# A down projection with 16 of its 22 chunks by a seven-product scheme

## The chip, the core and the metric

The kernel runs on one core of a Trainium2 chip. The metric is the time of one execution on the device, in microseconds. Three runs of the kernel before gave 772.88, 773.05 and 773.07 us, a median of 773.05.

## What is computed

One layer of a decoder trunk on 512 tokens of 1024 channels, in float32: a mixer with two branches, an output projection, and a dense gated feed-forward network (FFN). The change touches the last matrix product, `w_down` with 2816 rows and 1024 columns:

```python
def swiglu(h, w_gate, w_up, w_down):
    return (jax.nn.silu(h @ w_gate) * (h @ w_up)) @ w_down

    ...
    h = rmsnorm(x, ffn_pre_g[l])
    x = x + rmsnorm(swiglu(h, w_gate[l], w_up[l], w_down[l]), ffn_post_g[l])
```

## The kernel before

Every operand of a large product is split into a high half, which is the value rounded to the format `fp32r`, and a low half, the rest. A product is then three matmuls: high by high, high by low, low by high (`mm3`, lines 153 to 156). The high half is a copy on ScalarE (ACT in the profile; line 70) and the low half a subtraction on VectorE (DVE; line 71). Both stand in the helper `split`.

The FFN's gate and up product already runs by Strassen's scheme with seven products per quad of weight blocks (`jobs`, `prep_job`, `product`, lines 672 to 862). Sums of weight blocks are made there by accumulating DMAs, which POOL issues (`add_to`, line 692), and by additions on VectorE. Its result is `act`, 22 tiles of 128 rows by 512 tokens.

The down projection follows. It runs over 22 chunks `kc` of 128 rows of `w_down`. `unit("d", kc)` gives the halves of a chunk's weights (128 x 1024, tiles `whi` and `wlo`, four buffers each) and `halves(kc)` those of `act[kc]`. For each chunk, `down` (lines 938 to 941) does four blocks of 128 tokens by two halves of 512 columns by three matmuls, 24 in all, into eight PSUM banks `db`. The stationary operand is a 128 x 128 piece of the activations and the moving one 512 columns of weights. A product's weights are prepared three units ahead of it (`AHEAD`). Weights come in as `raw` tiles of 512 KB through SP's DMA queue, four buffers deep.

The last four chunks (`RES`) are kept whole, and their matmuls are done token block by token block, so that each block's finish runs beside the next block's matmuls: a square with a row sum on ScalarE, a product with the gain on VectorE, an inverse root by three Newton steps (`rsqrt`, lines 158 to 180; on POOL, for the last block on VectorE), a scalar_tensor_tensor that scales and adds the residual, and the DMA out.

Engines take their instructions in order. The order on each is set by a scheduler that works from the order of the code; only instructions marked by `keep_in_program_order` are bound to it. Tiles of a pool that is opened where another was closed wait for the old tiles' last users.

Of the kernel before, what the change touches and what calls it, by code (L numbers as in the profile page):

```python
# [31 lines left out]
def trunk(ctx: ExitStack, tc: tile.TileContext, x, xt, w_n, w_f, w_u, w_ga, w_gb, w_qk,  # L32
          w_o, w_gq, w_d, pcol, b_f, w_sp, rows, out):
# [896 lines left out]

# [3 lines left out]
    stage["pool"], stage["n"] = dn, 14  # L934
    x2 = {}
    db = [[bank(f"d{tb}{i}") for i in range(2)] for tb in range(NT)]

    def down(kc, tb, i, w):
        o = slice(tb * P, (tb + 1) * P)
        c = slice(i * HALF, (i + 1) * HALF)  # L940
        mm3(db[tb][i], ath[kc][:, o], atl[kc][:, o], w[0][:, c], w[1][:, c], kc == 0, kc == NF - 1)

    for kc in range(NF - RES):
        halves(kc)
        w = unit("d", kc)
        halves(kc + 1)
        if kc == 2:
            g_fpost = row(3, "g_fpost")
        if 4 <= kc < 4 + NT:
            tb = kc - 4  # L950
            x2[tb] = []
            for i in range(2):
                t = slot(f"x2{tb}{i}")
                nc.sync.dma_start(out=t, in_=x2d[tb * P:(tb + 1) * P, i * HALF:(i + 1) * HALF])
                x2[tb].append(t)
        for tb in range(NT):
            for i in range(2):
                down(kc, tb, i, w)
    for kc in range(NF - RES, NF):
        halves(kc)  # L960
    last = [unit("d", kc) for kc in range(NF - RES, NF)]
    for tb in range(NT):
        end = tb == NT - 1
# [1 line left out]
        ts_ = [slot(f"dg{tb}{i}") for i in range(2)]
        for i in range(2):
            for kc in range(NF - RES, NF):
                down(kc, tb, i, last[kc - NF + RES])
# [1 line left out]
            nc.scalar.activation(out=j, in_=db[tb][i], func=AF.Square, accum_out=ss[:, i:i + 1])  # L970
            if end and i:
                nc.scalar.activation(out=ts_[i], in_=db[tb][i], func=AF.Copy)
                nc.gpsimd.tensor_tensor(out=ts_[i], in0=ts_[i], in1=g_fpost[i], op=ALU.mult)
            else:
                nc.vector.tensor_tensor(out=ts_[i], in0=db[tb][i], in1=g_fpost[i], op=ALU.mult)
# [61 lines left out]
```

## Time and profile before

| | us |
|---|---|
| median of three runs | 773.05 |
| profiled execution | 774.62 |
| its span, first to last instruction | 772.9 |
| TensorE busy in it | 754.0 |
| VectorE busy | 454.7 |
| ScalarE busy | 341.1 |
| POOL busy | 137.8 |

The times of the trace run from 0 to the span's 772.9 us. The down projection's first matmul starts at 645.42 us and its last at 764.90. PE is TensorE's matmuls, PEld its weight loads. "Idle before" is the time that an engine stood still before an instruction, with what ended it. A matmul's duration contains its way through the array, so the time between two starts tells more than the duration.

### The profile page before, as it was taken

How to read it: one execution, taken by the hardware profiler on the slowest of the kernel's cores; microseconds unless marked ns; L12 is line 12 of the kernel's file. 1: busy time of each engine (PE TensorE's matmuls, PEld its weight loads, DVE VectorE, ACT ScalarE, POOL GpSimd, SP SyncE). 2: the span in 40 equal slices, each digit the busy share in tenths (PEclk: the TensorE clock that was granted, in tenths of full speed). 3: DMA queues.
4: the chain of work that ended last, by engine and by line, in shares of the span. 5: the costliest groups of instructions: out<-in, count | busy, mean ns of one | idle time of the engine just before them, and what ended most of it. 6: DMA issues, size and time to landing. Idle time of an engine off the chain costs nothing. (4 is left out here: it accounts for less than half of the span.)

```text
span 772.9 us, 11042 instructions
## 1 busy us (share of the span) xinstructions
PE 754.0 (98%) x4294; PEld 663.3 (86%) x4294; DVE 454.7 (59%) x718; ACT 341.1 (44%) x561; POOL 137.8 (18%) x213
## 2 busy tenths in 40 slices
PE   8999999999999989999998899999999999999996
PEld 6888778888888878888888799999999998888884
DVE  4647732244325566776589599887778766334415
ACT  5343662322235544555468464444444545233312
POOL 0103000022024254444133201001010000000013
PEclk9999999999999999999999999999999999999999
DMA  8625332222232222231678769776877317332202
GB/s 293 226 72 186 114 107 93 98 82 83 84 121 96 68 96 96 74 104 56 198 291 297 199 206 262 209 191 181 206 194 184 83 58 250 129 109 87 77 0 109
DMA packets 34451, 109.55 MB, mean 142 GB/s; under 512 B 4568, under 2 KB 4824, under 8 KB 34400
## 3 DMA queue, kind: packets, MB, share of 16 engines
q1 hardware_dynamic: 30352, 94.82, 35.8%
q0 software_dynamic: 3168, 11.54, 8.6%
q10 hardware_dynamic: 880, 2.51, 0.8%
q8 instruction: 33, 0.54, 0.3%
q14 instruction: 18, 0.15, 0.1%
HBM read 104.64 MB, written 4.21 MB: 141 GB/s over the span
## 5 line engine op out<-in xcount | busy, mean ns | idle before, releaser
L154 PE MATMUL d<-whi_d,ath 128*128 128x512 f32 x144 | 56.0, 389 | 0.0
L155 PE MATMUL d<-wlo_d,ath 128*128 128x512 f32 x144 | 56.0, 389 | 0.0
L156 PE MATMUL d<-whi_d,atl 128*128 128x512 f32 x144 | 56.0, 389 | 0.0
L496 POOL TENSOR_SCALAR dm<-cb,cq 128x128 f32<-128x128 f32 (+3 forms) x32 | 40.0, 1259 | 74.4 <-DMA cb<-cdr 70.4
L692 POOL DMA_DIRECT2D a<-in_w_gq x22 | 19.2, 872 | 166.2 <-DVE s L721 49.4
L70 ACT ACTIVATE whi<-raw_a 128x1024 fp32r<-128x1024 f32 x29 | 30.6, 1058 | 28.3 <-issue 12.8
L71 DVE TENSOR_TENSOR wlo<-raw_a,whi 128x1024 fp32r<-128x1024 f32 x29 | 35.4, 1221 | 7.8 <-ACT whi L70 7.8
L71 DVE TENSOR_TENSOR atl<-act,ath 128x512 fp32r<-128x512 f32 x22 | 14.8, 691 | 42.6 <-ACT ath L70 42.6
L70 ACT ACTIVATE whi<-a 128x1024 fp32r<-128x1024 f32 x26 | 27.5, 1059 | 25.7 <-PE Y L861 10.9
L71 DVE TENSOR_TENSOR wlo<-s,whi 128x1024 fp32r<-128x1024 f32 x22 | 26.9, 1224 | 15.8 <-ACT whi L70 15.8
L70 ACT ACTIVATE ath<-act 128x512 fp32r<-128x512 f32 x22 | 13.3, 627 | 50.8 <-PE d L155 50.8
L70 ACT ACTIVATE whi<-s 128x1024 fp32r<-128x1024 f32 x22 | 23.3, 1060 | 27.5 <-PE V L861 19.2
L71 DVE TENSOR_TENSOR wlo<-a,whi 128x1024 fp32r<-128x1024 f32 x26 | 31.7, 1221 | 4.2 <-ACT whi L70 4.1
L453 POOL TENSOR_TENSOR sga<-sga,ug 128x512 f32<-128x512 f32 x8 | 14.1, 1761 | 99.7 <-ACT sga L442 99.7
L154 PEld LDWEIGHTS d<-whi_d,ath 128*128 128x128 f32 x144 | 27.0, 188 | 5.6
L155 PEld LDWEIGHTS d<-wlo_d,ath 128*128 128x128 f32 x144 | 27.0, 188 | 5.6
L156 PEld LDWEIGHTS d<-whi_d,atl 128*128 128x128 f32 x144 | 27.0, 188 | 5.5
L71 DVE TENSOR_TENSOR wlo_o<-raw_o,whi_o 128x512 fp32r<-128x512 f32 x32 | 21.1, 685 | 13.2 <-ACT whi_o L70 13.1
L861 PE MATMUL X<-b21h,whi 128*128 128x256 f32 x88 | 25.5, 290 | 2.8 <-ACT s L876 2.7
L71 DVE TENSOR_TENSOR wlo_d<-raw_d,whi_d 128x1024 fp32r<-128x1024 f32 x18 | 22.1, 1225 | 10.4 <-ACT whi_d L70 10.4
L71 DVE TENSOR_TENSOR wlo_ga<-raw_ga,whi_ga 128x1024 fp32r<-128x1024 f32 x8 | 9.8, 1225 | 29.9 <-ACT whi_ga L70 16.9
L70 ACT ACTIVATE whi_o<-raw_o 128x512 fp32r<-128x512 f32 x32 | 18.9, 624 | 18.4 <-PE o L156 7.7
(316 smaller groups left out, 2590.7 us busy)
## 6 DMA issues: line engine op xcount, KB each, us to landing
raw_a<-in_w_gq SPq DMA_DIRECT2D x36, 512.0 KB, 4.8
a<-in_w_gq SPq DMA_DIRECT2D x22, 512.0 KB, 6.5
a<-in_w_gq POOLq DMA_DIRECT2D x22, 512.0 KB, 6.8
raw_d<-in_w_d SPq DMA_DIRECT2D x22, 512.0 KB, 3.4
raw_o<-in_w_o SPq DMA_DIRECT2D x16, 512.0 KB, 3.2
raw_va<-in_w_n SPq DMA_DIRECT2D x8, 512.0 KB, 6.0
raw_u<-in_w_u SPq DMA_DIRECT2D x8, 512.0 KB, 3.3
raw_ga<-in_w_ga SPq DMA_DIRECT2D x8, 512.0 KB, 3.2
```

Source lines behind the costliest of these rows:

```text
L70: keep(nc.scalar.activation(out=hi, in_=src, func=AF.Copy))
L71: keep(nc.vector.tensor_tensor(out=lo, in0=src, in1=hi.bitcast(F32), op=ALU.subtract))
L154: nc.tensor.matmul(ps_ap, lh, rh, start=first, stop=False)
L155: nc.tensor.matmul(ps_ap, lh, rl, start=False, stop=False)
L156: nc.tensor.matmul(ps_ap, ll, rh, start=False, stop=last)
L453: nc.gpsimd.tensor_tensor(out=sg, in0=sg, in1=ug[j], op=ALU.mult)
L496: nc.gpsimd.tensor_scalar(out=dm[:, :n], in0=cb[:, :n], scalar1=cq[:, i, h:h + 1], scalar2=None, op0=ALU.subtract)
L692: tc.keep_in_program_order(nc.gpsimd.dma_start(out=t, in_=quad_of(g, n_), accum_op=ALU.add))
L861: nc.tensor.matmul(o, l_[:, w_], r_[:, kc, :], start=start and pair + kc + m == 0, stop=pair == 1 and kc == 3 and m == 2, skip_group_check ...
```

## The change

Sixteen of the 22 chunks form four quads `q` of four chunks. In a quad, rows are halved (chunks 0 and 2 against 1 and 3), weight columns are halved (2 x 512), and tokens are halved (2 x 256). That gives weight blocks a11, a12, a21, a22 of 128 x 1024 each and activation blocks b11 to b22. A quad takes seven products of 12 matmuls each in place of 96 matmuls. The products go pass by pass: pass 1 for the quads 0 to 3, then passes 2, 6, 7 and 5; pass 3 alternates with the six plain chunks 16 to 21 (`"s"`), two of which stand alone after it; pass 4 comes last. Below, 6q3 is the product of pass 6 for quad 3.

- Sums of weights: `load_sums` loads a11 and a21 of a quad through SP and adds a22 onto a21 by an accumulating DMA that POOL issues. In pass 6 VectorE adds a21 + a22 and a11 to s2 (`s2d`), and POOL then issues a second accumulating DMA, a21 onto a11. Pass 3 adds a12 onto s2 on VectorE. Of each quad, eight transfers of 512 KB take the place of four.
- Sums of activations: VectorE, in pieces of 128 x 256, in place in `act` or in `t2`.
- Each product splits its activation block in two pieces of 256 columns (`th`, `tl`).
- Results go to four pairs of banks, V, X, Y and Z. `kept` copies V to SBUF on ScalarE after passes 1, 6 and 5; `combine` merges these with X, Y and Z on VectorE.
- The end: after the last plain chunk, token blocks 2 and 3 are finished while pass 4 runs; then `finish` of block 0 and of block 1. The resident four chunks are gone, and so is the split of the last block's finish over ScalarE and POOL.

```diff
-    ath, atl, dn = [None] * NF, [None] * NF, None
-
-    def halves(kc):
-        if kc < NF and ath[kc] is None:
-            ath[kc], atl[kc] = (dn.tile([P, S], F32R, tag=n_, bufs=6, name=f"{n_}{kc}") if dn else
-                                slot(f"{n_}{kc}", F32R) for n_ in ("ath", "atl"))
-            split(ath[kc], atl[kc], act[kc])
+    DQ = 4
+    order_d = [(p, q) for p in "12675" for q in range(DQ)]
+    rest = list(range(4 * DQ, NF))
+    for q in range(DQ):
+        order_d += [("s", rest[q]), ("3", q)]
+    order_d += [("s", kc) for kc in rest[DQ:]] + [("4", q) for q in range(DQ)]
...
+    def load_d(k):
+
+        if k < len(order_d) and k not in draw:
+            p, q = order_d[k]
+            src = {"1": "a11", "2": "a12", "3": "a12", "4": "a22"}
+            if p in src or p == "s":
+                draw[k] = st.tile([P, D], F32, tag="raw", bufs=NRAW, name=f"raw_d{p}{q}")
+                nc.sync.dma_start(out=draw[k], in_=w_d[q - 4 * DQ] if p == "s" else dquad(q, src[p]))
+
+    def load_sums(q):
+        if q < DQ:
+            for n_ in ("a11", "a21"):
+                dtile[q, n_] = dn.tile([P, D], F32, tag="dq", bufs=3 * DQ, name=f"{n_}d{q}")
+                nc.sync.dma_start(out=dtile[q, n_], in_=dquad(q, n_))
+            nc.gpsimd.dma_start(out=dtile[q, "a21"], in_=dquad(q, "a22"), accum_op=ALU.add)
+
+    def prep_unit():
...
+        for k_ in range(k, k + 4):
+            load_d(k_)
+        if p == "2":
+            load_sums(q + 2)
+        add = lambda out, a_, b_, o=ALU.add: nc.vector.tensor_tensor(out=out, in0=a_, in1=b_, op=o)
+        if p == "s":
+            th, tl = (pair_tile(n_, 3, f"{n_}{q}") for n_ in ("ath", "atl"))
+            split(th, tl, act[q])
+            src = draw[k]
+        else:
+            half = lambda c, j: act[4 * q + c][:, j * 2 * P:(j + 1) * 2 * P]
+            if p == "6":
+                dtile[q, "s2"] = dn.tile([P, D], F32, tag="dq", bufs=3 * DQ, name=f"s2d{q}")
+                add(dtile[q, "s2"], dtile[q, "a21"], dtile[q, "a11"])
+                nc.gpsimd.dma_start(out=dtile[q, "a11"], in_=dquad(q, "a21"), accum_op=ALU.add)
+                t2s[q] = dn.tile([P, S], F32, tag="t2", bufs=DQ, name=f"t2d{q}")
+            if p == "3":
+                add(dtile[q, "s2"], dtile[q, "s2"], draw[k])
...
+                if p == "6":
+                    t = t2s[q][:, o]
+                    nc.vector.scalar_tensor_tensor(out=t, in0=b11, scalar=-1.0, in1=b22,
+                                                   op0=ALU.mult, op1=ALU.subtract)
+                elif p == "7":
+                    add(b12, b12, b22, ALU.subtract)
+                elif p == "4":
+                    add(b21, b21, t2s[q][:, o])
+                split(th[:, o], tl[:, o], t)
+                if p == "2":
+                    add(b11, b11, b12, ALU.subtract)
+        hi = st.tile([P, D], F32R, tag="whi", bufs=4, name=f"whi_d{p}{q}")
+        lo = st.tile([P, D], F32R, tag="wlo", bufs=4, name=f"wlo_d{p}{q}")
+        split(hi, lo, src)
...
+    def d_part(k, i, q=None):
...
+        for r in range(2):
+            t_ = slice(r * 2 * P + i * P, r * 2 * P + (i + 1) * P)
+            w_ = slice(r * HALF, (r + 1) * HALF)
+            for m, (l_, r_) in enumerate(((th, wh), (th, wl), (tl, wh))):
+                nc.tensor.matmul(b, l_[:, t_], r_[:, w_], start=p in "127" and q + r + m == 0,
...
+    combine("s", X, ALU.add)
+    combine("v5", Z, ALU.add)
+    for i in range(2):
+        finish(2 + i, (lambda: V[i], lambda: held["v5"][i]), False)
+    while dstate["next"] < len(order_d):
+        prep_unit()
+    for i in range(2):
+        for k in range(first4, len(order_d)):
+            d_part(k, i)
+
+        def tail():
+            if not held.get(("done", i)):
+                add(held["v"][i], Y[i], held["v"][i], ALU.subtract)
+                held["done", i] = True
+            return held["v"][i]
+
+        finish(i, (lambda: held["s"][i], tail), i == 1)
```

Where the instructions stand. First POOL, from the FFN's last accumulating DMA on (`a` is an FFN weight tile, `v_d`, `y_d`, `w_d` and `t_d` are the inverse root's), before:

```order
L692 DMA a_5893<-in_w_gq 128x1024
L164 TENSOR_SCALAR v_d_7045<-sd_7012 128x1
L168 TENSOR_SCALAR y_d_7046<-v_d_7045 128x1
L170 TENSOR_SCALAR w_d_7047<-v_d_7045 128x1
L173 TENSOR_SCALAR t_d_7048<-y_d_7046,w_d_7047 128x1
```

and now, with the quads 0 to 3 as tiles 6380, 6385, 6424, 6453 of a21 and 6378, 6383, 6422, 6451 of a11:

```order
L685 DMA a_5893<-in_w_gq 128x1024
L905 DMA a21d_6380<-in_w_dq 128x1024
L905 DMA a21d_6385<-in_w_dq 128x1024
L905 DMA a21d_6424<-in_w_dq 128x1024
L927 DMA a11d_6378<-in_w_dq 128x1024
L927 DMA a11d_6383<-in_w_dq 128x1024
L905 DMA a21d_6453<-in_w_dq 128x1024
L927 DMA a11d_6422<-in_w_dq 128x1024
L927 DMA a11d_6451<-in_w_dq 128x1024
L157 TENSOR_SCALAR v_d_7244<-sd_7236 128x1
```

Eight accumulating DMAs now stand ahead of the first inverse root, and a21 of quad 3 stands behind a11 of quads 0 and 1.

VectorE in pass 6, now, from the low half of 2q3's weights to the low half of 6q3's (`wlo_d_6629`); before, this stretch held only low halves of weights and activations in turn:

```order
L71 TENSOR_TENSOR wlo_d_6517<-raw_d_6420,whi_d_6516 128x1024
L71 TENSOR_TENSOR tl_6537<-t2d_6535,th_6536 128x256
L917 TENSOR_TENSOR s2d_6532<-a21d_6380,a11d_6378 128x1024
L71 TENSOR_TENSOR tl_6537<-t2d_6535,th_6536 128x256
L917 TENSOR_TENSOR s2d_6560<-a21d_6385,a11d_6383 128x1024
...
L917 TENSOR_TENSOR s2d_6616<-a21d_6453,a11d_6451 128x1024
L71 TENSOR_TENSOR tl_6621<-t2d_6619,th_6620 128x256 x2
L71 TENSOR_TENSOR tl_6645<-act_3734,th_6644 128x256
L71 TENSOR_TENSOR tl_6645<-act_3801,th_6644 128x256
L71 TENSOR_TENSOR wlo_d_6629<-s2d_6616,whi_d_6628 128x1024
```

The sum `s2d_6616` of quad 3 and four short subtractions stand ahead of 6q3's low half.

VectorE at the end, before, from the last low half of weights (`wd_7009`) on:

```order
L71 TENSOR_TENSOR wd_7009<-raw_d_6874,wd_7009 128x1024
L71 TENSOR_TENSOR atl_7002<-act_6118,ath_7001 128x512
L71 TENSOR_TENSOR atl_7006<-act_6291,ath_7005 128x512
L975 TENSOR_TENSOR dg_7013<-d_6370,g_fpost_6452 128x512
L975 TENSOR_TENSOR dg_7014<-d_6371,g_fpost_6454 128x512
L982 SCALAR_TENSOR_TENSOR dg_7013<-dg_7013,y_d_7046,x_6524 128x512
```

and now, with 4q3's low half as `wlo_d_7295`:

```order
L1053 TENSOR_TENSOR dg_7262<-v5d_6908,g_fpost 128x512
L1053 TENSOR_TENSOR dg_7262<-Vd_6389,g_fpost 128x512
L1058 SCALAR_TENSOR_TENSOR dg_7237<-dg_7237,y_d_7245,x_7128 128x512 x2
L1058 SCALAR_TENSOR_TENSOR dg_7262<-dg_7262,y_d_7270,x_7070 128x512 x2
L71 TENSOR_TENSOR wlo_d_7295<-raw_d_7130,whi_d_7294 128x1024
L1053 TENSOR_TENSOR dg_7323<-sd_6504,g_fpost 128x512
L1053 TENSOR_TENSOR dg_7373<-sd_6505,g_fpost 128x512
L867 TENSOR_TENSOR vd_6716<-Yd_6392,vd_6716 128x512
L1053 TENSOR_TENSOR dg_7323<-vd_6716,g_fpost 128x512
L1058 SCALAR_TENSOR_TENSOR dg_7323<-dg_7323,y_d_7332,x_7230 128x512 x2
L867 TENSOR_TENSOR vd_6717<-Yd_6393,vd_6717 128x512
```

The last low half of weights stood ahead of every finish; now it stands behind the finish of token blocks 2 and 3 (`dg_7237`, `dg_7262`), and block 1's subtraction (`vd_6717`) stands behind block 0's finish.

TensorE in pass 4, now, where bank 6392 is token block 0's and 6393 block 1's; 18 matmuls of 4q0 to 4q2 into bank 6392 stand ahead of these:

```order
L1009 MATMUL Yd_6392<-whi_d_7294,th_7286 128x512
L1009 MATMUL Yd_6393<-whi_d_7140,th_7132 128x512
L1009 MATMUL Yd_6393<-wlo_d_7141,th_7132 128x512
L1009 MATMUL Yd_6393<-whi_d_7140,tl_7133 128x512
L1009 MATMUL Yd_6393<-whi_d_7140,th_7132 128x512
L1009 MATMUL Yd_6393<-wlo_d_7141,th_7132 128x512
L1009 MATMUL Yd_6393<-whi_d_7140,tl_7133 128x512
L1009 MATMUL Yd_6393<-whi_d_7164,th_7156 128x512
L1009 MATMUL Yd_6392<-wlo_d_7295,th_7286 128x512
L1009 MATMUL Yd_6392<-whi_d_7294,tl_7287 128x512
```

So 26 matmuls of pass 4 come before the first that reads `wlo_d_7295`.

## Rows read from the trace of the kernel before

**Rows 1.** The page's part 1: busy time, share of the span, instructions.

```profile
PE 754.0 (98%) x4294; PEld 663.3 (86%) x4294; DVE 454.7 (59%) x718; ACT 341.1 (44%) x561; POOL 137.8 (18%) x213
```

**Rows 2.** The page's part 4: the chain that ended last, by engine.

```profile
PE 42%; DVE 1%; ACT 0%; issue 0%; DVEq 0%; ACTq 0%
PE V L861 13%; PE Y L861 8%; PE d L156 5%; PE d L155 5%; PE d L154 5%; PE X L861 4%; ACT whi L70 0%; DVE s L757 0%; DVE s L721 0%; DVE wlo L71 0%; DVEq L1033 0%; DVE t_d L173 0%; ACT dsq L970 0%; DVE y_d L174 0%; DVE dg L982 0%
```

**Rows 3.** Timeline of TensorE, first and last of 528 matmuls: start, duration, instruction.

```profile
645.42 0.40 PE L154 MATMUL d<-whi_d,ath 128*128 128x512 f32 x1
...
764.90 0.39 PE L156 MATMUL d<-wd,atl 128*128 128x512 f32 x1
```

**Rows 4.** Busy time by stretch: length, engines' times, clock, DMA share, GB/s.

```profile
645.40:667.20 21.80, 21.80 (x98) 18.05 (x97) 10.24 (x13) 8.22 (x13) 0.00 (x0) 1.00 0.67 240
```

**Rows 5.** Groups by form, VectorE and ScalarE, 640 to 773: busy us, mean ns.

```profile
L71 DVE TENSOR_TENSOR wlo_d<-raw_d,whi_d 128x1024 fp32r<-128x1024 f32 x17 | 20.8, 1225 | 9.1 <-ACT whi_d L70 9.1
L982 DVE SCALAR_TENSOR_TENSOR dg<-dg,y_d,x 128x256 f32<-128x256 f32 x2 | 0.9, 480 | 0.0
L70 ACT ACTIVATE whi_d<-raw_d 128x1024 fp32r<-128x1024 f32 x17 | 17.8, 1050 | 8.8 <-PE d L156 4.4 <-issue 2.6 <-ACT ath L70 1.8
```

**Rows 6.** Timeline of VectorE at the projection's start, back to back.

```profile
646.64 1.23 DVE L71 TENSOR_TENSOR wlo_d<-raw_d,whi_d 128x1024 fp32r<-128x1024 f32 x1 [0.33 <-ACT whi_d L70]
647.78 0.42 DVE L871 TENSOR_TENSOR act<-v,si 128x256 f32<-128x256 f32 x1
648.12 2.49 DVE L71 TENSOR_TENSOR atl<-act,ath 128x512 fp32r<-128x512 f32 x4
```

**Rows 7.** DMA from 457 to 458: queue, packets, MB, share of 16 engines.

```profile
q1 hardware_dynamic: 107, 0.40, 100.1%
```

**Rows 8.** DMA from 463 to 464, accumulating transfers alone.

```profile
q0 software_dynamic: 48, 0.20, 101.0%
```

**Rows 9.** Timeline of SP's queue: the sixth load for the projection.

```profile
642.13 3.20 SPq L120 DMA_DIRECT2D raw_d<-in_w_d  x2
```

**Rows 10.** DMA issued from 642 to 643: count, KB each, us to landing.

```profile
raw_d<-in_w_d SPq DMA_DIRECT2D x1, 512.0 KB, 3.2
```

**Rows 11.** Line 692, all accumulating DMAs: ns of an issue, us to landing.

```profile
L692 POOL DMA_DIRECT2D a<-in_w_gq x22: 853/862/1097, 428.2 to 612.4; - x22
...
DMA to landing us min/median/max: 5.2/6.8/9.5
```

**Rows 12.** Timeline of ScalarE, POOL and VectorE: finish of token block 0.

```profile
749.00 0.60 ACT L970 ACTIVATE dsq<-d 128x512 f32<-128x512 f32 x1 [2.03 <-PE d L156]
749.50 0.20 ACT L970 ACTIVATION_READ_ACCUMULATOR dsq<-d 128x1 f32 x1
749.80 0.29 POOL L164 TENSOR_SCALAR v_d<-sd 128x1 f32<-128x1 f32 x1 [136.51 <-ACT dsq L970]
753.03 1.42 DVE L982 SCALAR_TENSOR_TENSOR dg<-dg,y_d,x 128x512 f32<-128x512 f32 x2 [2.61 <-POOL y_d L174]
```

**Rows 13.** Timeline of ScalarE and VectorE: finish of the last block.

```profile
765.38 0.60 ACT L970 ACTIVATE dsq<-d 128x512 f32<-128x512 f32 x1 [2.09 <-PE d L156]
766.10 0.21 DVE L164 TENSOR_SCALAR v_d<-sd 128x1 f32<-128x1 f32 x1 [0.20 <-ACT dsq L970]
768.28 1.54 DVE L982 SCALAR_TENSOR_TENSOR dg<-dg,y_d,x 128x512 f32<-128x512 f32 x3
```

**Rows 14.** Busy time by stretch, columns as in rows 4, after the last matmul.

```profile
769.00:770.00 1.00, 0.00 (x0) 0.00 (x0) 0.82 (x3) 0.00 (x0) 0.00 (x0) 1.00 0.11 43
770.00:771.00 1.00, 0.00 (x0) 0.00 (x0) 0.00 (x0) 0.00 (x0) 0.00 (x0) 0.66 1.00 353
771.00:772.00 1.00, 0.00 (x0) 0.00 (x0) 0.00 (x0) 0.00 (x0) 0.00 (x0) 0.50 0.39 128
```

**Rows 15.** DMA issued from 464 to 465, behind accumulating ones.

```profile
raw_a<-in_w_gq SPq DMA_DIRECT2D x1, 512.0 KB, 11.3
```

More of the change, by code (lines that the diff above doesn't have):

```diff
@@ L105, in trunk @@
     NRAW = 4
-    RES = 4
     def fetch():
@@ L933, in trunk @@
     dn = dnx.enter_context(tc.tile_pool(name="dn", bufs=1, reuse_waits="tile"))
[L934 to L963, printed above, removed]
+    for q in range(2):
+        load_sums(q)
+    V, X, Y, Z = ([bank(f"{n_}d{i}") for i in range(2)] for n_ in "VXYZ")
+    acc = {"1": V, "6": V, "5": V, "3": V, "2": X, "7": Y, "4": Y}
+    def d_part(k, i, q=None):
+        p, q = order_d[k]
+        wh, wl, th, tl = dready[k]
+        b = acc[p][i]
+        for r in range(2):
+            t_ = slice(r * 2 * P + i * P, r * 2 * P + (i + 1) * P)
+            w_ = slice(r * HALF, (r + 1) * HALF)
+            for m, (l_, r_) in enumerate(((th, wh), (th, wl), (tl, wh))):
+                nc.tensor.matmul(b, l_[:, t_], r_[:, w_], start=p in "127" and q + r + m == 0,
+                                 stop=(p in "34" and q == DQ - 1 or q == DQ - 1) and r == 1 and m == 2,
+                                 skip_group_check=True)
@@ new lines, in d_plain @@
+    def d_plain(k):
+        kc = order_d[k][1]
+        wh, wl, th, tl = dready[k]
+        for banks, tb0, i in ((X, 0, 0), (Z, 2, 1), (Y, 0, 1), (V, 2, 0)):
+            for j in range(2):
+                t_, w_ = slice((tb0 + j) * P, (tb0 + j + 1) * P), slice(i * HALF, (i + 1) * HALF)
+                for m, (l_, r_) in enumerate(((th, wh), (th, wl), (tl, wh))):
+                    nc.tensor.matmul(banks[j], l_[:, t_], r_[:, w_],
+                                     start=banks is Z and kc == rest[0] and m == 0,
+                                     stop=m == 2, skip_group_check=True)
@@ new lines, in trunk, with kept, combine, row_tile @@
+    held = {}
+    def kept(name, banks):
+        held[name] = [slot(f"{name}d{i}") for i in range(2)]
+        for t, b in zip(held[name], banks):
+            copy(t, b)
+    def combine(name, banks, op):
+        for t, b in zip(held[name], banks):
+            add(t, b, t, op)
+    rows_d = {}
+    def row_tile(name):
+        return dn.tile([P, D], F32, tag="dq", bufs=3 * DQ, name=name)
+    def load_rows(tb):
+        rows_d[tb] = row_tile(f"x2{tb}")
+        nc.sync.dma_start(out=rows_d[tb], in_=x2d[tb * P:(tb + 1) * P, :])
@@ L964, in trunk, with finish @@
+    def finish(tb, parts, end):
         ss = small(f"sd{tb}", 2)
[L965 to L968, printed above, removed]
+        dg, x2r = row_tile(f"dg{tb}"), rows_d[tb]
+        for i, src in enumerate(parts):
+            c = slice(i * HALF, (i + 1) * HALF)
             j = slot(f"dsq{tb}{i}")
[L970 to L975, printed above, removed]
+            nc.scalar.activation(out=j, in_=src(), func=AF.Square, accum_out=ss[:, i:i + 1])
+            nc.vector.tensor_tensor(out=dg[:, c], in0=src(), in1=g_fpost[:, c], op=ALU.mult)
```

76 lines of the change are left out of this document (52 added, 24 removed).

## The prediction

> **What bounds the kernel now.** The page's first part comes first: TensorE is busy for 98% of the span [rows 1]. The chain of waits then says that this is the bound: 42% of the span is TensorE on the chain itself, and among the lines on it are the gate and up product (L861) and the down projection (L154 to L156) [rows 2]. I then read the timeline of the down projection. It starts with its first 512-column matmul at 645.42 and its last at 764.90, right behind the last FFN product; 528 matmuls stand in it, so one every 119.48 / 527 = 0.2267 us, with no gap [rows 3]. In its first 21.8 us, in which the changed kernel does its first eight units, VectorE works 10.2 us and the DMA engines are two thirds busy [rows 4]. So a matmul less is worth 0.2267 us there, as long as the operands still arrive in time, and everything below asks whether they do.
>
> **What goes.** Four quads of 12 matmuls per product and seven products make 336, six plain chunks 6 x 24 = 144: 480 in place of 528. 48 x 0.2267 = **10.9 us** less. The three forms, their tile sizes and their order within a triple are those of before, so I keep the pitch.
>
> **Elementwise work.** From the groups and the pitch at which instructions follow each other [rows 5, 6], a 1024-column subtraction takes VectorE 1.14 us, a 512-column operation 0.6, one of 256 columns 0.34 and a scalar_tensor_tensor of 256 columns 0.4. Each quad unit needs 1.14 + 2 x 0.34 = 1.82 us. In the four passes 1, 2, 6 and 7 stand 16 units (29.1 us), 16 additions of 256 columns (5.4), eight scalar_tensor_tensor (3.2) and four sums of 1024 (4.6): 42.3 us, against 16 x 12 x 0.2267 = 43.5 us of TensorE. It is covered, but by 1.2 us, and that only because an operand's buffers (four deep) let it be made three units ahead. I take nothing for it, and 2 us as the upper end. From pass 5 on there is slack: 3.2 us of VectorE per pair of plain chunk and product is well under 8.2 us of TensorE. ScalarE, with 1.0 us and two short copies per unit [rows 5], never limits.
>
> **First wait: the sums of weights.** Pass 6 of quad 3 needs a21 + a22 of that quad, which POOL's queue makes with an accumulating DMA, and VectorE adds a11 to it. One plain 512 KB transfer uses all DMA engines for 0.524 / 0.40 = 1.31 us [rows 7], an accumulating one for 0.524 / 0.20 = 2.62 us [rows 8]. Now count what is queued before that sum is done. The first six loads are issued as before; the sixth, 2q1's, goes out at 642.13 [rows 9], and from it on the queue no longer runs empty. A load alone needs 3.2 us to land [rows 10], so 2q1's data begin to move at 642.13 + 3.2 - 1.31 = 644.0. Plain loads: 2q1 to 2q3, eight of a11 and a21, and four for chunks 16 and 17 and pass 3 (their buffers come free with the subtractions of pass 2, by about 661): 15 x 1.31 = 19.7 us. Accumulating ones: POOL's order has a21 of quads 0, 1, 2, then a11 of 0 and 1, then a21 of quad 3: 6 x 2.62 = 15.7. The two of a11 wait for VectorE's sums s2 of quads 0 and 1. Those stand behind the halves of 2q2 and 2q3, which stand behind ScalarE's copies of V, and these can't start before pass 1 ends at 645.42 + 48 x 0.2267 = 656.3; copies, halves and additions put s2 of quad 1 at about 664.5. So the last sum is issued behind everything else, at about 666, and its data are through at 644.0 + 35.4 = 679.4, landed at about 679.8. Then VectorE's sum (1.2), and in parallel ScalarE's high half (1.05) and four short subtractions of VectorE (1.3), then the low half (1.2): 683.5. TensorE wants that low half for its second matmul of unit 6q3, at 645.42 + 133 x 0.2267 = 675.6. **Wait: 7.9 us.** Bounds: with a landing 5.2 us after an issue at 666, the shortest of the 22 [rows 11], the halves are ready at 675.0, and the wait is nothing; with rates a tenth lower it is 11.5. I take 7.9: before had one such pile, of three accumulating transfers, and there a plain load took 11.3 us to land [rows 15]; this pile is twice as long. Pass 7 follows on: its sums land at 674 to 686, each before its unit, so no second wait there.
>
> The Trainium skill (SBUF — State Buffer, SBUF: two separate sides) warns that POOL cannot write the descriptors of its DMAs while VectorE holds their shared port. By that rule each of these issues could be late by one VectorE operation, 1.2 us, and the wait 9.1. The trace does not bear it out: the 22 issues took 853 to 1097 ns, median 862 [rows 11], beside a busy VectorE, so the sum leaves it out.
>
> **Restart.** After the last matmul of before, TensorE's granted clock was 1.00 until about 770.3 and then 0.50, so it fell from 2.4 to 1.2 GHz some 5 us after work stopped [rows 14]. In the first wait TensorE idles 6.5 us before its first matmul of 6q3, so it should restart at 1.2 GHz. What a restart costs isn't in the trace; at half clock a unit of 12 takes 2.7 us more. From 0 to 2.7 I take the middle, **1.4**.
>
> The Trainium skill (TensorE: Matmul & The Clock Gate, What's actually happening) says that an idle TensorE falls to half rate and needs sustained work to come back. The fall agrees with rows 14; no row shows the way back. By that rule the end of 0 falls away, and the sum below would lie between it and 2.7 us more; it goes by the middle all the same.
>
> **Second wait and the end.** Call T0 the end of the last plain chunk. Behind it TensorE has 26 matmuls before it needs the low half of 4q3 (the order above): 5.9 us. VectorE has that subtraction behind the two finishing steps of token blocks 2 and 3, and each of those waits for an inverse root on POOL. From T0: squares on ScalarE (0.7 each, the first from T0 - 0.4), so POOL starts at 1.1; POOL's chain takes 3.23 [rows 12], twice, to 7.5; two scalar_tensor_tensor (1.4) to 8.9; the subtraction to 10.1. **TensorE waits 4.2 us.** Five matmuls and their drain: 11.4. Then block 0: subtraction 0.8, square 0.7, POOL 3.2, two scalar_tensor_tensor 1.4, to 17.6. VectorE takes block 1's subtraction only behind these, though TensorE is done at 15.3: 18.3; square 0.7 to 19.0; inverse root on VectorE 2.2, two scalar_tensor_tensor 1.4, and 3.1 from the last of them to the end of the span [rows 13]: 25.7. After TensorE's end that is 10.4 us; before it was 772.9 - 765.3 = 7.6. **Tail: +2.8.** What bounds this pair is POOL's 3.23, which is measured; I allow 0.7 either way on the 7.0.
>
> **Sum.** -10.9 + 7.9 + 1.4 + 4.2 + 2.8 = +5.4 us. The profiled execution took 774.62 us with a span of 772.9; the median of the runs is 773.05. The span goes to 778.3, the median to **778.5**, if what lies around the span stays.
>
> **Rivals.** *The sums land in time.* Were POOL's transfers served ahead of the plain ones, or the DMA engines faster together than rows 7 and 8 say, the first wait and the restart are gone. The two ends of the down projection remain: -10.9 + 7.0 = -3.9, 769.2 us, faster. It decides at a landing of quad 3's sum by 672; for it speaks the 5.2 us, against it that 35 us of transfers lie in 28 us. *A half wait.* With POOL's share served first, the plain load of a21 of quad 3 comes late instead, and the sum lands at 675 to 677: wait 3 to 5 us, restart up to 1, so -10.9 + 7.0 + 3 to 6: 772.2 to 775.2. *The pile-up spreads.* If rates fall by a tenth, VectorE's thin cover breaks in pass 7, and the clock stays low for a unit more than I took: 11.5 + 2 + 4 in place of 9.3, 786.7.
>
> **How the numbers follow.** Forecast 0.62 (775 to 783); sums in time 0.12; half wait 0.14; spread 0.12. A measurement of this kernel can tell about 0.2%, 1.5 us, from no change. Slower by more: the forecast, the spread and a little under half of the half waits, 0.80; within: 0.08; faster: 0.12. The range leaves out the faster rival and the far end of the spread: 772 to 785.
>
> **What would show it.** Right: TensorE idle 6 to 9 us before its first matmuls of pass 6, quad 3, put down to an ACT or DVE half, with quad 3's accumulating DMA landing 12 us or more after its issue; DMA busy share near 1 from 645 to 680; a second gap of about 4 us near the end, released by DVE's last low half; 10 us from the last matmul to the end. Wrong: no gap in pass 6, a pitch other than 0.227, or a last low half that does not wait for POOL.

## The result and the profile after

Four runs of the changed kernel took 782.49, 782.58, 785.10 and 785.14 us, a median of 783.84; four of the kernel before, on the same chip, 773.02. The ratio is 1.0131, with a 95% interval of 1.0114 to 1.0147: slower, by 10.8 us. The forecast was 778.5, 5.5 us slower. The profiled execution took 782.58 us with a span of 780.9.

TensorE worked less, as meant, and the rest is standing still. Against [rows 1] its busy time is 7 us lower and its share has fallen; against [rows 2] the chain that ended last now runs through DMA, POOL and VectorE. The page's part 1 and the first line of its part 4, after:

```profile
PE 746.9 (96%) x4246; PEld 655.6 (84%) x4246; DVE 501.4 (64%) x818; ACT 364.8 (47%) x618; POOL 145.3 (19%) x220
PE 35%; DMA 4%; DVE 2%; POOL 1%; issue 1%; ACT 1%; DVEq 0%; POOLq 0%; ACTq 0%
```

TensorE's waits from 630 us on (before had none there): who waited for whom, us in total, times, longest.

```profile
PE Vd L1009 <- ACT whi_d L70: 5.9, 2, 5.1
PE Yd L1009 <- DVE wlo_d L71: 5.2, 1, 5.2
PE Vd L1009 <- DVE wlo_d L71: 1.4, 2, 0.8
```

They lie in the two places that the prediction names. The first is pass 6, quads 2 and 3 (timeline of TensorE, columns as in [rows 3], with the idle time before an instruction in brackets):

```profile
670.94 0.39 PE L1009 MATMUL Vd<-whi_d,tl 128*128 128x512 f32 x1
672.14 0.50 PE L1009 MATMUL Vd<-whi_d,th 128*128 128x512 f32 x1 [0.81 <-ACT whi_d L70]
673.45 0.50 PE L1009 MATMUL Vd<-wlo_d,th 128*128 128x512 f32 x1 [0.80 <-DVE wlo_d L71]
...
675.83 0.39 PE L1009 MATMUL Vd<-whi_d,tl 128*128 128x512 f32 x1
681.33 0.79 PE L1009 MATMUL Vd<-whi_d,th 128*128 128x512 f32 x1 [5.11 <-ACT whi_d L70]
682.72 0.80 PE L1009 MATMUL Vd<-wlo_d,th 128*128 128x512 f32 x1 [0.60 <-DVE wlo_d L71]
683.32 0.63 PE L1009 MATMUL Vd<-whi_d,tl 128*128 128x512 f32 x1
...
687.29 0.39 PE L1009 MATMUL Yd<-whi_d,th 128*128 128x512 f32 x1
```

The projection's first matmul started at 643.94. The one at 687.29 is the first of pass 7; 144 stand ahead of it and would have taken 144 x 0.2267 = 32.6 us, to 676.6: passes 1, 2 and 6 lost 10.7 us. Behind the wait the matmuls are longer, 0.63 us, and the granted clock is 0.50 from 681 to 686.5, the lower of the two levels, 1.2 GHz (last row of the stretches below).

The chain of waits shows what stood behind it (start, us, what):

```profile
651.18 11.02 DMA a21d<-in_w_dq
662.23 1.23 DVE s2d L917
663.75 0.17 POOL a11d L927
664.41 14.53 DMA a21d<-in_w_dq
680.11 1.24 DVE tl L71 x4
681.45 1.23 DVE wlo_d L71
```

Quad 3's accumulating transfer was issued at 664.41 and landed 14.5 us later; the 22 of [rows 11] took 5.2 to 9.5. Stretch by stretch (columns as in [rows 4]) the DMA engines were full from 645 to 675, with shares of 1.03 and 1.05; before, the first 21.8 us of the projection had 0.67:

```profile
645.00:660.00 15.00, 15.00 (x68) 12.42 (x67) 15.00 (x30) 10.68 (x23) 1.73 (x2) 1.00 1.03 324
660.00:675.00 15.00, 13.39 (x58) 10.53 (x58) 8.31 (x13) 5.63 (x11) 4.38 (x5) 1.00 1.05 303
675.00:690.00 15.00, 9.29 (x30) 6.84 (x29) 11.04 (x21) 8.21 (x14) 0.86 (x1) 0.77 0.82 186
...
681.00:686.50 5.50, 4.57 (x10) 3.29 (x11) 5.50 (x10) 4.36 (x7) 0.35 (x1) 0.50 0.81 177
```

The second place is unit 4q3, after the last plain chunk (timelines of TensorE and of VectorE):

```profile
758.24 0.39 PE L1009 MATMUL Yd<-whi_d,th 128*128 128x512 f32 x1
763.80 0.80 PE L1009 MATMUL Yd<-wlo_d,th 128*128 128x512 f32 x1 [5.17 <-DVE wlo_d L71]
764.39 0.63 PE L1009 MATMUL Yd<-whi_d,tl 128*128 128x512 f32 x1
...
771.08 0.39 PE L1009 MATMUL Yd<-whi_d,tl 128*128 128x512 f32 x1
```

```profile
757.22 1.41 DVE L1058 SCALAR_TENSOR_TENSOR dg<-dg,y_d,x 128x512 f32<-128x512 f32 x2 [2.52 <-POOL y_d L167]
761.20 1.42 DVE L1058 SCALAR_TENSOR_TENSOR dg<-dg,y_d,x 128x512 f32<-128x512 f32 x2 [2.56 <-POOL y_d L167]
762.53 1.22 DVE L71 TENSOR_TENSOR wlo_d<-raw_d,whi_d 128x1024 fp32r<-128x1024 f32 x1
...
772.46 0.68 DVE L867 TENSOR_TENSOR vd<-Yd,vd 128x512 f32<-128x512 f32 x1
```

The low half of 4q3 stands behind the scalings of token blocks 2 and 3, and each of those waited for an inverse root on POOL. The two roots took 3.7 and 4.0 us; two of their small operations, which take 0.29 and 0.22 us in the kernel before (timeline of POOL):

```profile
753.50 0.78 POOL L157 TENSOR_SCALAR v_d<-sd 128x1 f32<-128x1 f32 x1 [72.15 <-ACT dsq L1052]
757.99 0.72 POOL L163 TENSOR_SCALAR w_d<-v_d 128x1 f32<-128x1 f32 x1
```

In the kernel before, VectorE's only operation beside the root of [rows 12] had an operand in PSUM, `d`:

```profile
749.73 0.69 DVE L975 TENSOR_TENSOR dg<-d,g_fpost 128x512 f32<-128x512 f32 x1 [2.03 <-ACT dsq L970]
```

Now 7.8 us went here, 5.3 of them waiting and the rest at half clock.

**One measure for all kernels.** The first matmul of the down projection starts at 643.6 to 646.8 us in the profiled executions of these kernels, though all of them do the same work up to there, and the fast runs of the kernel before themselves lie between 772.77 and 776.49 us. So the table gives, beside each median, the time from that first matmul to the end of the span. "Pass 6" is the time from the first matmul to the first one behind pass 6, and "4q3" that from the first matmul of pass 4 to the last, each less 0.2267 us per matmul.

| kernel | median us | from first matmul to end | pass 6 | 4q3 |
|---|---|---|---|---|
| before | 773.02 | 127.5 | 0 | 0 |
| changed | 783.84 | 136.9 | 10.7 | 7.8 |
| again | 784.02 | 137.0 | 10.8 | 8.0 |
| a21_first | 780.73 | 133.9 | 7.7 | 8.2 |
| pass6_order | 778.90 | 132.8 | 6.2 | 6.7 |
| late_plain | 778.72 | 132.9 | 6.5 | 8.1 |
| plain_dmas | 776.00 | 129.0 | 1.8 | 7.3 |
| halves_first | 782.38 | 134.8 | 11.2 | 0 |
| roots_side | 779.93 | 133.2 | 11.0 | 0 |
| tail_order | 778.01 | 132.3 | 10.9 | 0 |
| no_gains | 779.25 (one run) | 130.8 | 10.9 | 0 |
| all | 770.23 | 124.4 | 1.9 | 0 |
| best | 768.96 | 123.5 | 2.1 | 0 |
| best2 | 767.40 | 121.4 | 1.4 | 0 |

### The profile page after: what moved, and what is told of

The parts are those of the page before. It is cut to its first block, busy times and chain, and to the rows that moved or that the text cites. A ratio compares the mean times of both kernels' runs of the same rounds, so it can differ in the third digit from the quotient of the medians.

```text
span 780.9 us, 11146 instructions
## 1 busy us (share of the span) xinstructions
PE 746.9 (96%) x4246; PEld 655.6 (84%) x4246; DVE 501.4 (64%) x818; ACT 364.8 (47%) x618; POOL 145.3 (19%) x220
## 5 line engine op out<-in xcount | busy, mean ns | idle before, releaser
L489 POOL TENSOR_SCALAR dm<-cb,cq 128x128 f32<-128x128 f32 (+3 forms) x32 | 40.0, 1260 | 74.3 <-DMA cb<-cdr 32.6
L70 ACT ACTIVATE whi<-a 128x1024 fp32r<-128x1024 f32 x26 | 27.5, 1058 | 25.8 <-PE Y L853 10.9
L1009 PE MATMUL Vd<-whi_d,th 128*128 128x512 f32 x64 | 26.1, 409 | 5.9 <-ACT whi_d L70 5.9
L71 DVE TENSOR_TENSOR wlo_gb<-raw_gb,whi_gb 128x1024 fp32r<-128x1024 f32 x8 | 9.8, 1226 | 28.5 <-ACT whi_gb L70 15.5
L1009 PE MATMUL Vd<-wlo_d,th 128*128 128x512 f32 x64 | 26.0, 406 | 1.4 <-DVE wlo_d L71 1.4
L147 PE MATMUL vs<-whi_vs,xgh 128*128 128x512 f32 x64 | 24.9, 391 | 1.3 <-ACT whi_vs L70 1.3
L853 PE MATMUL V<-t2h,whi 128*128 128x256 f32 x88 | 25.0, 284 | 0.8 <-ACT whi L70 0.8
L1009 PE MATMUL Vd<-whi_d,tl 128*128 128x512 f32 x64 | 25.6, 400 | 0.0
L147 PE MATMUL o<-whi_o,mgh 128*128 128x512 f32 x64 | 25.6, 400 | 0.0
L147 PE MATMUL ga<-hth,whi_ga 128*128 128x512 f32 x64 | 25.5, 399 | 0.0
L148 PE MATMUL o<-wlo_o,mgh 128*128 128x512 f32 x64 | 25.4, 398 | 0.0
```

The costliest lines, as they stand in the source:

```text
L70: keep(nc.scalar.activation(out=hi, in_=src, func=AF.Copy))
L71: keep(nc.vector.tensor_tensor(out=lo, in0=src, in1=hi.bitcast(F32), op=ALU.subtract))
L147: nc.tensor.matmul(ps_ap, lh, rh, start=first, stop=False)
L148: nc.tensor.matmul(ps_ap, lh, rl, start=False, stop=False)
L489: nc.gpsimd.tensor_scalar(out=dm[:, :n], in0=cb[:, :n], scalar1=cq[:, i, h:h + 1], scalar2=None, op0=ALU.subtract)
L853: nc.tensor.matmul(o, l_[:, w_], r_[:, kc, :], start=start and pair + kc + m == 0, stop=pair == 1 and kc == 3 and m == 2, skip_group_check ...
```

## Experiments

The first set asks which of the two places costs what, and by which mechanism.

**again**: the changed kernel, unaltered.

> The changed kernel once more, unaltered. Its four runs fell on two times, 782.5 and 785.1 us, and the forecast has no term for the 2.6 us between them. Theory 1 (a clock restart): in one of the two stretches behind a wait, 681 to 690 or 764 to 771 us, TensorE stays at the lower level for about one unit of 12 matmuls more, which costs 2.7 us. Theory 2 (the pile of transfers): quad 3's sum lands at about 681.6 in place of 679.0 and the wait in pass 6 is 2.6 us longer. If this profile is of the longer time, it shows which; if not, only that the two times come back.

The profile is 137.0 us long from the first matmul, a tenth more than the first one, with 10.8 and 8.0 us lost in the two places; only its start was 1.4 us later. Neither theory was seen. The profiles of these kernels differ by up to 3 us in where the projection starts, so the 2.6 us between the two times are of the size of a difference that arises before it, and the kernel before has runs as far apart. No profile shows the longer time, so this stays an inference. The clock behaved differently, though. Busy time by stretch:

```profile
675.00:678.50 3.50, 3.50 (x9) 2.71 (x10) 0.00 (x0) 0.00 (x0) 0.00 (x0) 0.53 1.06 211
679.00:682.00 3.00, 0.32 (x2) 0.00 (x0) 1.82 (x4) 0.56 (x1) 0.30 (x1) 1.00 0.88 173
682.50:688.00 5.50, 4.86 (x11) 3.52 (x12) 5.50 (x10) 4.21 (x7) 0.07 (x1) 0.50 0.87 188
```

Here unit 6q2 itself ran at half clock (0.53) after idle times of 0.9 and 0.8 us. That cost nothing: the slower unit ended later, and the wait for quad 3's sum was shorter by as much.

**a21_first**

```diff
-            nc.gpsimd.dma_start(out=dtile[q, "a21"], ... accum_op=ALU.add)
+            tc.keep_in_program_order(nc.gpsimd.dma_start(out=dtile[q, "a21"], ... accum_op=ALU.add))
...
-                nc.gpsimd.dma_start(out=dtile[q, "a11"], ... accum_op=ALU.add)
+                tc.keep_in_program_order(nc.gpsimd.dma_start(out=dtile[q, "a11"], ... accum_op=ALU.add))
```

> Only POOL's queue changes: the four a21 + a22 sums stand ahead of all a11 sums, where before the a11 sums of quads 0 and 1 stood ahead of the a21 sum of quad 3. Theory A (the forecast's: the transfers pile up): 2 x 2.62 = 5.2 us of accumulating transfers go behind quad 3's sum, which lands at about 673.7 in place of 679.0; its low half is ready at 677.4, TensorE waits about 3 us in pass 6 in place of 8.6, too short for the clock to fall; the a11 sums then land one every 2.6 us from 676.5 and cost pass 7 0 to 2 us. Time 774 to 777 us against 783.8. Rival B (a transfer that POOL issues is late by itself, some 14.5 us from issue to landing whatever is queued): the issue moves from 664.4 to about 662, the landing to 676.5, the wait shrinks by 2.4 us and the restart stays: 780 to 782 us.

Quad 3's sum landed 30.5 us after the first matmul in place of 35.0, 4.5 us earlier, 9.4 us after its issue: theory A's mechanism. But the time from the first matmul fell by 3.0 us, not 7 or more. VectorE's timeline says why:

```profile
675.51 1.22 DVE L917 TENSOR_TENSOR s2d<-a21d,a11d 128x1024 f32<-128x1024 f32 x1 [1.94 <-DMA a21d<-in_w_dq]
676.66 1.22 DVE L71 TENSOR_TENSOR wlo_d<-s2d,whi_d 128x1024 fp32r<-128x1024 f32 x1
```

The second row is quad 2's low half. The scheduler had put it behind quad 3's sum, so both quads waited for the last transfer. And the clock fell, behind waits of 1.7 and 3.3 us that theory A had called too short for it; that cost 2.2 us.

**plain_dmas**

```diff
-            nc.gpsimd.dma_start(out=dtile[q, "a21"], in_=dquad(q, "a22"), accum_op=ALU.add)
+            nc.gpsimd.dma_start(out=dtile[q, "a21"], in_=dquad(q, "a22"))
```

and the same for a11.

> The eight transfers that POOL issues overwrite their tile in place of adding to it, so the sums of weights are left out; everything else stays. Theory A (an accumulating transfer takes the DMA engines twice as long, 2.62 against 1.31 us): the six ahead of TensorE's need give back 6 x 1.31 = 7.9 us, quad 3's tile lands at about 671, no wait is left in pass 6, nor the restart: 10.7 us less, 773 us against 783.8. Rival B (what makes them slow is that POOL issues them, through its own queue): quad 3's tile still lands at 677 to 679 and the time stays within 2 us.

Quad 3's tile landed 28.1 us after the first matmul, which stood at 645.10, 7.0 us earlier (timeline of VectorE):

```profile
673.16 1.23 DVE L917 TENSOR_TENSOR s2d<-a21d,a11d 128x1024 f32<-128x1024 f32 x1 [1.68 <-DMA a21d<-in_w_dq]
```

Pass 6 lost 1.8 us in place of 10.7. Theory A: the double price of an accumulating transfer, from [rows 7, 8], gave 7.9 us and 7.0 came. Rival B, no change, is out: transfers that POOL issues are not slow by that alone.

**halves_first**

```diff
-        while dstate["next"] <= min(k + AHEAD, len(order_d) - 1):
+        while dstate["next"] <= min(k + AHEAD + (k == first4 - 1), len(order_d) - 1):
...
+        if (p, q) == ("4", DQ - 1):
+            hi, lo = (row_tile(f"{n_}_d43").bitcast(F32R) for n_ in ("whi", "wlo"))
```

> The halves of unit 4q3 get a pair of buffers of their own and are made before the finish of token blocks 2 and 3. Theory A (TensorE's wait is the loss): the 5.3 us of waiting and the 2.7 us at half clock behind it go, 8.1 us in all: 775 to 776 us against 783.8. Rival B (the finish is the bound, by the same POOL steps): TensorE ends 8 us earlier, at about 763.4, but block 1's subtraction still stands on VectorE behind the scalings of blocks 2, 3 and 0, which wait for three inverse roots of 3.23 us on POOL one after the other; block 0's last scaling ends at about 769.8 in place of 772.5, and only 2.7 us are won: 781 us. TensorE's end and the idle time before VectorE's last subtraction tell them apart.

TensorE's delay at 4q3 is gone, all 7.8 us, and its last matmul starts 119.8 us after the first, against 127.1. The end came only 2.1 us earlier: rival B, which said 2.7. The chain at the end:

```profile
764.49 1.41 DVE dg L1061 x2
767.11 0.61 DVE vd L867
768.56 0.30 POOL v_d L157
771.78 1.42 DVE dg L1061 x2
773.19 0.61 DVE vd L867
```

Block 1's subtraction (773.19) still stands behind block 0's scaling, which waits for POOL. TensorE had been done for over 6 us.

The second set takes the two places further.

**pass6_order**: a21_first, with the additions and halves of pass 6 on VectorE marked `keep_in_program_order` too.

> As a21_first, and VectorE's pass 6 is bound to the order low half of quad 2, then sum s2 of quad 3 (in a21_first the scheduler had turned these round, so that quad 2's low half stood behind a sum that waited for the DMA). Times below are from the first matmul of the down projection. Theory A (the forecast's pile, and an order that a21_first had made for itself): quad 2's sum lands at 26.7, its low half is ready at 30.3 where TensorE wants it at 27.4; quad 3's lands at 30.5, its low half is ready at 34.5, wanted by then at 33.1: 4 to 5 us of waiting in two pieces, 0 to 2 of half clock; 2 to 3 us less than a21_first, 131 to 132 us from the first matmul to the end against 133.9. Rival B (the order costs nothing, the landing alone counts): no change from a21_first, 133 to 134.

Pass 6 lost 6.2 us: 3.2 in waits, where a21_first had 5.4, and 3.0 at half clock, for which theory A had allowed 2 at most. So the order did cost 2.2 us of waiting, the clock took back a part, and the whole came to 132.8, just above A's range.

**late_plain**

```diff
+                if 5 * DQ <= k < 6 * DQ:
+                    draw[k] = dn.tile([P, D], F32, tag="dq", bufs=3 * DQ, name=f"raw_d{p}{q}")
...
+                if k >= 5 * DQ:
+                    tc.keep_in_program_order(ins)
```

> Only the plain loads of chunks 16 to 19 and of pass 3 are held back: the first four go into tiles that come free in passes 7 and 5, the others stay behind them in SP's queue. POOL's queue stays as it was. Theory A (all transfers share one pile): four plain loads of 1.31 us leave it, quad 3's sum lands 5.2 us earlier, 29.8 us after the first matmul of the down projection in place of 35.0; its low half is ready at 33.5 against 30.1 wanted; the wait falls from 8.6 to about 3.4 and the restart from 2.1 to between 0 and 2: 130 to 132 us from the first matmul to the end, against 137.0. Rival B (POOL's queue and SP's queue do not hold each other up): the landing stays at 34 to 35 and the time at 136 to 137.

The sum landed at 30.5, 4.5 us earlier; the wait fell from 8.6 to 4.1 and the unit behind it ran at half clock: 132.9, a little above A's range, 4.0 us less than the changed kernel. VectorE took the sum at 676.96, the first matmul being at 646.47:

```profile
676.96 1.23 DVE L922 TENSOR_TENSOR s2d<-a21d,a11d 128x1024 f32<-128x1024 f32 x1 [4.17 <-DMA a21d<-in_w_dq]
```

In the changed kernel four transfers on another queue, for products that began 30 us after the sum's landing, had held it up. The two queues draw on one supply.

**roots_side**: halves_first, `e = nc.vector if end or tb == 3 else nc.gpsimd`, and block 3 finished first.

> As halves_first, and the inverse root of token block 3 goes from POOL to VectorE, block 3 being finished ahead of block 2. Theory A (at the end the three inverse roots on POOL, one after the other, are the bound): POOL has two chains of 3.2 us in place of three; VectorE's subtraction for block 1 starts 13 us after the last plain chunk in place of 17.2; 130 to 131 us from the first matmul to the end against 134.8. Rival B (VectorE's own queue is the bound): its instructions grow by a root of 2.2 us, and the end comes at 134 to 136.

133.2: neither. POOL had two roots in place of three, but VectorE, which takes its work in order, stood still in the middle of block 3's root until POOL had block 2's:

```profile
760.55 0.75 DVE L1061 SCALAR_TENSOR_TENSOR dg<-dg,y_d,x 128x512 f32<-128x512 f32 x1 [2.58 <-POOL y_d L167]
```

The subtraction for block 0, at 762.98, stood behind that. So the question became one of order.

**tail_order**: halves_first, with the finish cut into two functions and VectorE's operations at the end marked `keep_in_program_order`, in this order: scaling of block 2, block 0's subtraction and gains, scaling of block 3, block 1's subtraction, scaling of block 0, block 1's gains, root and scaling.

> As halves_first, all inverse roots as there (three on POOL, the last on VectorE), and VectorE's order at the end is bound: scaling of block 2, subtraction and gains for block 0, scaling of block 3, subtraction for block 1, scaling of block 0, gains and root of block 1. Nothing is added or taken away. Theory A (what bound halves_first and roots_side was VectorE's order, in which the subtractions for blocks 0 and 1 stood behind scalings that wait for POOL): block 1's subtraction comes right behind TensorE's last matmul, 11 us after the last plain chunk in place of 17.2, then the scaling of block 0 (1.4 us) and block 1's root: 128 to 129 us from the first matmul of the down projection to the end, against 134.8. Rival B (the three roots on POOL, one after the other, are the bound whatever the order): 133 to 135 us.

132.3, nearer to B. Block 1's subtraction now came at 763.82, right behind TensorE, but then VectorE waited for the third root on POOL until 766.4. Order and roots bind together. And POOL's roots took 4.0, 4.9 and 4.0 us, where [rows 12] had shown 3.23. The two timelines side by side, POOL first:

```profile
753.53 0.77 POOL L157 TENSOR_SCALAR v_d<-sd 128x1 f32<-128x1 f32 x1 [72.62 <-ACT dsq L1067]
759.17 0.33 POOL L166 TENSOR_SCALAR t_d<-y_d,w_d 128x1 f32<-128x1 f32 x1
759.61 1.23 POOL L167 TENSOR_SCALAR y_d<-t_d,y_d 128x1 f32<-128x1 f32 x1
```

```profile
758.90 0.69 DVE L1104 TENSOR_TENSOR vd<-Yd,vd 128x512 f32<-128x512 f32 x1
759.50 0.68 DVE L1068 TENSOR_TENSOR dg<-sd,g_fpost 128x512 f32<-128x512 f32 x1
760.10 0.69 DVE L1068 TENSOR_TENSOR dg<-vd,g_fpost 128x512 f32<-128x512 f32 x1
```

POOL's operation of 759.61, 0.27 us long elsewhere, lasted until VectorE's two multiplications were over.

**no_gains** tests that.

```diff
-            K(nc.vector.tensor_tensor(out=dg[:, c], in0=src(), in1=g_fpost[:, c], op=ALU.mult))
+            if tb < 2:
+                K(nc.vector.tensor_tensor(out=dg[:, c], in0=src(), in1=g_fpost[:, c], op=ALU.mult))
```

> tail_order with the multiplications by the gain left out for token blocks 2 and 3 (that part of the result is not computed); nothing else moves. In tail_order these four ran on VectorE from 752.8 to 755.3, beside the first root on POOL, which took 4.0 us against 3.2 in the kernel before. Theory A (a small POOL operation that starts while VectorE works on a 512-column one waits for its end): the first root takes 3.2 us, with 0.29 us for its first operation in place of 0.77; the second and third, beside block 2's and block 3's scaling and block 0's operations, stay near 4.9 and 4.0. Rival B (it is the first POOL operation after an idle stretch that is slow): 0.77 for the first operation and 4.0 us for the root, as before.

The scalings of blocks 2 and 3 then read their operand directly, V from PSUM. Theory A. The first root took 3.17 us, from 756.54 to the next one's start at 759.71, with 0.29 for its first operation after 72 us of rest; the second and third took 4.7 and about 3.7:

```profile
756.54 0.29 POOL L157 TENSOR_SCALAR v_d<-sd 128x1 f32<-128x1 f32 x1 [72.08 <-ACT dsq L1067]
759.71 0.29 POOL L157 TENSOR_SCALAR v_d<-sd 128x1 f32<-128x1 f32 x1
```

**all**, **best** and **best2** put the pieces together. all is pass6_order, late_plain and roots_side, with the passes in the order 1, 2, 6, 5, 7; best takes tail_order's end; best2 puts block 3's root on VectorE at a fixed place, one gain of block 1 on POOL, and block 0's scaling ahead of block 1's root.

```diff
-    order_d = [(p, q) for p in "12675" for q in range(DQ)]
+    order_d = [(p, q) for p in "12657" for q in range(DQ)]
...
-                combine("v5", Y, ALU.subtract)
+            elif p == "7":
+                combine("v5", Y, ALU.subtract)
```

> All of it together (a21 sums first with VectorE's order bound, the plain loads late, the halves of 4q3 early, block 3's root on VectorE), and pass 5 goes ahead of pass 7, so that the a11 sums have 11 us more. Theory A: only 15 - 4 = 11 plain and 4 accumulating transfers stand before quad 3's sum, 24.9 us of them, landed at 25.5 against 26.6 wanted: 0 to 1 us of waiting, 480 x 0.2267 = 108.8 us of matmuls and 10.5 us of tail: 119 to 121 us from the first matmul to the end against 127.5 of the kernel before, 766 us or 1% faster. Rival B (VectorE becomes the bound of passes 2 and 6 once the DMA is not: 42.3 us of work in 43.5): 2 to 4 us of short waits, 122 to 125 us, 769 us.

> The kernel called all, with the roots and the bound order of tail_order in place of block 3's root on VectorE. Theory A: the 2 us of short waits in pass 6 stay, 110.9 us from the first to behind the last matmul, and the tail is 8 to 9 us in place of 13.6: 119 to 120 us from the first matmul to the end against 127.5 of the kernel before, 764 to 766 us. Rival B (the order at the end is not the bound): 123 to 125 us as in all, 769 to 770 us.

> As best, with the inverse root of block 3 on VectorE in a fixed place (behind the gains of blocks 2 and 3, and block 3's scaling right behind it), so that POOL has the roots of blocks 2 and 0 alone; one gain of block 1 goes to POOL, and block 0's scaling stands between block 1's subtraction and its root. Theory A (in best the end is bound by three roots on POOL, which took 4.0, 4.9 and 4.0 us there): block 1's root starts 13.2 us after the last plain chunk in place of 16.2, and the end follows 6.9 us behind its start: 120 to 121 us from the first matmul of the down projection to the end against 123.5, 765 to 767 us. Rival B (VectorE has no room for a second root while TensorE does pass 4): 122.5 to 124 us, 768 to 769 us.

In all, pass 6 lost 1.9 us, between theory A's 0 to 1 and rival B's 2 to 4: two waits for VectorE's low halves, with VectorE itself waiting 1.0 us for quad 2's sum ahead of them, and one for ScalarE's copy of V, which pass 5 needs right behind pass 6. The clock stayed at 1.00. But the tail was 13.4 us, not 10.5: 124.4, 770.23 us against 772.89, a ratio of 0.9957 (0.9940 to 0.9974). best came to 123.5, rival B's number: with three roots on POOL at 4.0, 4.9 and 4.0 us in place of two, the bound order won 0.9 us. best2 came to 121.4, between A's 121 and B's 122.5: 767.40 against 774.57, a ratio of 0.9910 (0.9893 to 0.9928), faster than both kernels. VectorE's end in best2:

```profile
754.35 0.69 DVE L1121 TENSOR_TENSOR vd<-Yd,vd 128x512 f32<-128x512 f32 x1 [0.98 <-PE Yd L1020]
758.22 0.20 DVE L157 TENSOR_SCALAR v_d<-sd 128x1 f32<-128x1 f32 x1
```

Block 1's subtraction waits for TensorE now, as it should, but its root starts 3.2 us behind it. Between them stand the rest of POOL's second root and block 0's scaling, and that took 2.4 us, 1.0 more than in the other kernels, beside the gain that I had moved to POOL (VectorE's row, then POOL's):

```profile
755.90 2.40 DVE L1063 SCALAR_TENSOR_TENSOR dg<-dg,y_d,x 128x512 f32<-128x512 f32 x2 [0.86 <-POOL y_d L167]
755.83 1.26 POOL L1079 TENSOR_TENSOR dg<-vd,g_fpost 128x512 f32<-128x512 f32 x1
```

That move cost more than the 0.6 us it took off VectorE. Of the 10.9 us that the scheme saves, 6.1 are kept.

## Why the prediction was right or wrong

- **What goes, right.** From 687.29 to 758.24 lie 313 pitches of 0.2267 us. The 48 matmuls gave 10.9 us.
- **Elementwise work, right.** Passes 1 and 2 show no gap. In best2, with most of the pile out of the way, pass 6 loses 1.4 us, inside the 0 to 2 that was kept: 0.7 in a wait for VectorE's low half of 6q3 and 0.5 in one for ScalarE's copy of V. VectorE had stood 0.55 us for quad 2's transfer just ahead, so what its thin cover costs by itself isn't shown.
- **First wait, right in mechanism and nearly in size.** The sum landed 35.0 us after the first matmul; the forecast had 34.4. The low half of 6q3 came 8.6 us late; the forecast had 7.9. It came in two pieces, 2.2 us at 6q2 and the rest at 6q3, where the forecast had one. a21_first, late_plain and plain_dmas each took transfers out of the pile and moved the landing by 4.5, 4.5 and 7.0 us, where its prices gave 5.2, 5.2 and 7.9. So the pile is shown; its rates were some 12% off in that direction. The first sign that it named for being right held only with both pieces: 5.7 us of idling before the first two matmuls of 6q3, 7.3 with those of 6q2, for "6 to 9". The rivals "sums in time" and "half wait" fell, and so did "the pile-up spreads": pass 7 shows no gap. The issue was at 664.4, as forecast (666, less the 1.5 us by which the projection started earlier), and it landed 14.5 us later, not 5.2.
- **Restart, mis-sized.** 1.4 was taken, the middle of 0 and 2.7; 2.1 was measured: one pitch of 0.60 us and eight of 0.43, in place of 0.23.
- **Second wait, mis-sized twice.** 5.3 us in place of 4.2. The two roots on POOL took 3.7 and 4.0 us, not 3.23 each. In [rows 12] VectorE worked on an operand in PSUM for the first 0.6 us of the root and then stood idle; here it was multiplying and scaling beside the roots with both operands in SBUF (last section). And the wait was followed by a restart of its own, 2.5 us, for which the sum has no term; the prediction gives no reason, but its 4.2 us lie under the "some 5 us" of [rows 14]. The clock was down after 5.2 us here, and also after 2.8 us in late_plain and after two waits under 1 us in again. That one row of a fall was not enough to say when it doesn't happen.
- **Tail.** 9.4 us in place of 10.4, because TensorE ended late. From the last plain chunk (752.6) to the end the forecast had 25.7 us and 28.3 were measured; 1.3 of the 2.6 are POOL's slower roots and about 1.0 the five matmuls at half clock ahead of block 0's subtraction.
- **The sum.** +9.4 us from the first matmul to the end, against +5.4: 1.4 in pass 6, 3.6 at 4q3, 1.0 given back in the tail. 773.0 + 9.4 is 782.4, near the lower two of the four runs; what made the other two 2.6 us longer isn't settled. The median, 783.84, lies inside the range of 772 to 785, but 0.8 us above the 775 to 783 of the forecast itself, and two of the four runs lie 0.1 us outside the range. What the range kept its upper end for, the spreading pile, is not what took the time there: it was the second wait and its restart.
- **What the forecast saw without using it.** It said that POOL's 3.23 us bound the last two terms together. halves_first and tail_order showed how much: taking TensorE's whole 7.8 us away returned 2.1, since the finishes stand in one line on POOL and on VectorE.

## What to carry to other kernels

A saving on a full engine is worth what its operands' supply allows: add up the transfers between the moment the buffers come free and the first use, at their measured rates and over all queues, and put what is wanted first at the head, across queues too. At the end of a kernel follow the last results through every engine's own order before you price a wait on the engine you look at: a wait that runs beside a longer chain gives little back. A duration read while its neighbour is idle, or out of its way, is a lower bound.
